# First stage of a hybrid diffusion layer on one core: the modulation from plain fp32 products, latents shifted and scaled by rows before the transposes, tokens loaded in between

## The chip, the cores and the metric

The kernel runs on one core of a Trainium2 chip. The metric is device time in microseconds of one execution; the smaller the better. The core's engines are TensorE (PE in the views), VectorE (DVE), ScalarE (ACT), GpSimd (POOL) and the queue SP, which in this kernel issues nearly all transfers. Each engine works its instructions off in the order in which they were built into its queue.

## What is computed

One layer of a bidirectional diffusion backbone over 2048 latent tokens and 256 context tokens of width 1024. The part that matters here is the very first:

```python
c_act, cctx_act = silu(c), silu(c_ctx)
mod_lat = c_act @ ada_w + ada_b            # 6 x 1024, shift and scale are the first two parts
mod_ctx = cctx_act @ ada_w + ada_b
h_ctx = rmsnorm(ctx, norm1_g) * (1 + csc1) + csh1
h_lat = rmsnorm(x + pos, norm1_g) * (1 + sc1) + sh1
proj  = h @ w_in                           # for both, then three groups of heads, a gated residual and an MLP
```

Everything behind `proj` (recurrent, linear-attention and mLSTM heads, output projection, MLP) makes up the other nineteen twentieths of the time and is not touched.

## The kernel before

All is fp32. To multiply exactly enough with TensorE's fast fp32 form (`F32R`), an operand is split into a part rounded to that form and the rest, and three products stand for one: `hTh` and `hTl` are the two parts of the normalised, modulated and transposed tokens, `whi` and `wlo` those of a weight block.

The stage before the heads runs like this. `csp` holds the two activated condition vectors (latents, context) in split form. For 8 row blocks k and 4 column blocks j a piece `aw` (128x512) of `ada_w` is loaded through SP into one of 8 slots (L271); ScalarE casts it to `awh` (L274), VectorE or GpSimd subtracts to get `awl` (L275), and two products (L276, L277) add it up in four PSUM banks `mps[j]`. The results are copied out as `mrow` and transposed, so that shift (`mT`) and scale (`sc1`) stand as one column for each of 8 blocks of 128 features.

Tokens come in 18 tiles of 128: two of the context (group 0) and four for each of the latent groups 1 to 4. `norm_in` loads a tile `xt` into one of 4 slots, adds the position for latents on GpSimd (`prow` in L237, `posc` in L238), sums squares on ScalarE (`junk`, L251), gets the reciprocal root from a few one-column operations (L215 to L225) and scales the tile on VectorE (L253). `modulate` transposes it in two halves of four blocks into PSUM `tp` (L444), applies scale and shift block by block into `hy`, five blocks of a tile on VectorE (L448) and three on ScalarE (L450), casts `hy` to `hTh` on ScalarE (L451) and subtracts to get `hTl`, one half on VectorE and one on GpSimd (L452).

TensorE's order is written out by hand: between the tiles a filler puts products of an earlier group (`first0` to `first4`, two weight blocks each, L365 to L367), some 2.7 us of them after each tile; `first4` stands behind all tiles. After it the first block of the long projection, `xa1`, begins. On the other engines a scheduler orders by data and by priorities (`tc.high_priority`); the modulation pieces have the highest. The weights of `first` (`wraw`, `whi`, `wlo`) are split on VectorE in the same stage.

## Time and profile before

| | |
|---|---|
| median of 3 runs | 2755.17 us (2750.44 to 2756.03) |
| the profiled execution: time | 2759.21 us |
| its span | 2757.4 us |
| busy in the span: TensorE, VectorE, ScalarE, GpSimd | 93%, 63%, 42%, 35% |
| the stage that is changed | about the first 150 us |

The shares are means over stages with different limits: TensorE's 93% says what bounds the kernel as a whole, not what bounds its first 150 us. The profiled execution is one run of the program, a little above the median; durations are taken from it, and a shift worked out from them is set against the median.

### The profile page before, as it was taken

Reading aid. Unit: us, or ns where it says so; the run is one execution under the profiler, and the core shown is the slowest. Engines: PE = TensorE matmul, PEld = TensorE weight load, DVE = VectorE, ACT = ScalarE, POOL = GpSimd, SP = SyncE. Lnnn points to the kernel's source line nnn. Section 1 sums busy time; section 2 is a strip of 40 time slices with the busy share of each in tenths; the row PEclk is TensorE's granted clock in tenths of the full one; section 3 lists DMA queues with packets and bytes.
Section 4 is the critical chain, followed back from the end, with each engine's and each line's share of the span. In section 5 each row is a group of like instructions: output and inputs, shape, how many; then the busy total and the mean of one; then the engine's idle time right before and its main releaser. Section 6 shows DMA issues by size and latency. Waiting matters only on the chain. (4 is left out here: it accounts for less than half of the span.)

```text
span 2757.4 us, 36372 instructions
## 1 busy us (share of the span) xinstructions
PE 2551.9 (93%) x12239; PEld 2074.5 (75%) x12239; DVE 1743.9 (63%) x3040; ACT 1159.9 (42%) x2052; POOL 972.6 (35%) x868
## 2 busy tenths in 40 slices
PE   5799999999998889788997999999999999999997
PEld 2677778888877667776775888878887887888876
DVE  7855476156648876746665776766665256555586
ACT  6746421233336665433334544544445322232343
POOL 5734411245444443424452333243331222222221
PEclk8999999999999999889998999999999999999999
DMA  7444365665656565856663776665555576656564
GB/s 222 143 133 120 99 183 168 167 156 162 159 156 172 169 188 176 275 182 207 209 203 115 207 221 203 197 192 145 157 149 158 186 263 224 212 179 198 171 206 153
DMA packets 490215, 495.24 MB, mean 180 GB/s; under 512 B 88226, under 2 KB 371580, under 8 KB 490028
## 3 DMA queue, kind: packets, MB, share of 16 engines
q1 hardware_dynamic: 464204, 465.45, 56.1%
q10 hardware_dynamic: 20352, 15.86, 1.8%
q0 software_dynamic: 5472, 11.60, 1.5%
q8 instruction: 97, 1.59, 0.2%
q14 instruction: 90, 0.74, 0.1%
HBM read 336.89 MB, written 155.92 MB: 179 GB/s over the span
## 5 line engine op out<-in xcount | busy, mean ns | idle before, releaser
L365 PE MATMUL pp<-hTh,whi 128*128 128x512 f32 (+1 forms) x1048 | 433.7, 414 | 12.8 <-DVE evt L505 8.8
L367 PE MATMUL pp<-hTh,wlo 128*128 128x512 f32 (+1 forms) x1048 | 406.4, 388 | 6.0 <-POOL wlo L313 3.9
L366 PE MATMUL pp<-hTl,whi 128*128 128x512 f32 (+1 forms) x1048 | 405.0, 386 | 0.2 <-DVE hTl L452 0.2
L1806 PE MATMUL yps<-bh,al 128*128 128x512 f32 x832 | 326.9, 393 | 6.6 <-DVE al L1425 3.5
L1804 PE MATMUL yps<-bh,ah 128*128 128x512 f32 x832 | 325.8, 392 | 0.0
L1805 PE MATMUL yps<-bl,ah 128*128 128x512 f32 x832 | 324.5, 390 | 0.0
L1425 POOL TENSOR_TENSOR al<-ar,ah 128x1024 fp32r<-128x1024 f32 x54 | 132.1, 2445 | 485.3 <-ACT ah L1666 448.6
L1666 ACT CAST ah<-ar 128x1024 fp32r<-128x1024 f32 x108 | 113.5, 1051 | 305.6 <-PE yps L1805 264.7
L365 PEld LDWEIGHTS pp<-hTh,whi 128*128 128x128 f32 x1048 | 203.5, 194 | 50.1 <-DVE evt L505 10.9
L367 PEld LDWEIGHTS pp<-hTh,wlo 128*128 128x128 f32 x1048 | 202.3, 193 | 49.8 <-POOL wlo L313 6.3
L366 PEld LDWEIGHTS pp<-hTl,whi 128*128 128x128 f32 x1048 | 203.5, 194 | 33.4 <-issue 1.9
L1806 PEld LDWEIGHTS yps<-bh,al 128*128 128x128 f32 x832 | 156.3, 188 | 46.5 <-DVE al L1425 8.5
L1805 PEld LDWEIGHTS yps<-bl,ah 128*128 128x128 f32 x832 | 156.3, 188 | 33.4
L1804 PEld LDWEIGHTS yps<-bh,ah 128*128 128x128 f32 x832 | 156.5, 188 | 31.9
L1498 PE MATMUL accy<-th,whi 128*128 128x512 f32 x384 | 153.1, 399 | 2.0 <-DVE tz L1428 1.9
L1500 PE MATMUL accy<-th,wlo 128*128 128x512 f32 x384 | 151.8, 395 | 1.6 <-DVE wlo L1425 1.6
L1425 DVE TENSOR_TENSOR wlo<-wab,whi 128x512 fp32r<-128x512 f32 x124 | 128.8, 1039 | 37.3 <-ACT whi L1433 37.3
L1499 PE MATMUL accy<-tl,whi 128*128 128x512 f32 x384 | 150.5, 392 | 0.0
L1433 ACT CAST whi<-wab 128x512 fp32r<-128x512 f32 x124 | 76.8, 620 | 131.9 <-PE accy L1499 57.4
L1428 POOL TENSOR_TENSOR uz<-tz 128x512 f32<-128x512 f32 x32 | 50.0, 1566 | 224.8 <-DVE tz L1428 144.6
L313 POOL TENSOR_TENSOR wlo<-wraw,whi 128x512 fp32r<-128x512 f32 x54 | 78.2, 1450 | 143.8 <-ACT whi L312 134.8
L1498 PE MATMUL pp<-th,whi 128*128 128x512 f32 x256 | 104.9, 410 | 15.9 <-ACT whi L1433 12.8
(407 smaller groups left out, 6008.5 us busy)
## 6 DMA issues: line engine op xcount, KB each, us to landing
uD<-uz SPq DMA_DIRECT2D x224, 256.0 KB
ar<-uD SPq DMA_DIRECT2D x108, 512.0 KB
braw<-in_mlp_w_dram SPq DMA_DIRECT2D x84, 512.0 KB
wab<-in_mlp_w_dram SPq DMA_DIRECT2D x62, 512.0 KB
maw<-in_ada_w_dram SPq DMA_DIRECT2D x64, 256.0 KB
wraw<-in_w_in_dram SPq DMA_DIRECT2D x54, 256.0 KB
rb<-rD SPq DMA_DIRECT2D x96, 128.0 KB
aw<-in_ada_w_dram SPq DMA_DIRECT2D x32, 256.0 KB
```

The lines of the kernel that those rows point to most:

```text
L313: (nc.vector if early else nc.gpsimd).tensor_tensor(lo, raw, hi.bitcast(F32), op=ALU.subtract)
L365: nc.tensor.matmul(acc[:, 0:n], hi, hTh[g][:, k, :], start=k == 0, stop=False)
L366: nc.tensor.matmul(acc[:, 0:n], hi, hTl[g][:, k, :], start=False, stop=False)
L367: nc.tensor.matmul(acc[:, 0:n], lo, hTh[g][:, k, :], start=False, stop=k == KC - 1)
L1425: eng.tensor_tensor(o, a, b, op=ALU.subtract)
L1498: nc.tensor.matmul(acc, hi[:, k, :], T2[i][0][:, k, :], start=first and k == 0, stop=False, skip_group_check=True)
L1499: nc.tensor.matmul(acc, hi[:, k, :], T2[i][1][:, k, :], start=False, stop=False, skip_group_check=True)
L1500: nc.tensor.matmul(acc, lo[:, k, :], T2[i][0][:, k, :], start=False, stop=k == 3, skip_group_check=True)
L1666: nc.scalar.copy(hi, r_)
L1804: nc.tensor.matmul(acc, ah[:, p_, :], bh, start=p_ == 0, stop=False)
L1805: nc.tensor.matmul(acc, ah[:, p_, :], bl, start=False, stop=False)
L1806: nc.tensor.matmul(acc, al[:, p_, :], bh, start=False, stop=p_ == 7)
```

## The change

The products of the modulation take `aw` as it is, in plain fp32, two columns of `cact` against 512 of `aw`; the split and `csp` go. The bias and the 1 of `1 + scale` are put in by four more products of a row of ones with the row `arow`. For the latents, shift and scale are taken as rows out of `mps` (the scale times `norm1_g`), spread over 128 partitions by four products of `ones1` with a row, and kept as `shB` and `scB`. A latent tile is then scaled and shifted before its transposes, by two operations of 128x1024 on VectorE, and `hTh` and `hTl` are taken straight out of PSUM, `hTl` on VectorE in both halves. For the context nothing changes in kind but its place: the tiles now come in the order of groups 1, 0, 2, 3, 4. The loads and norms of the first four tiles stand between the `aw` pieces from k = 2 on, with their priority.

```diff
-    csp = const.tile([P, KC, 4], F32R, name="csp")
-    nc.vector.tensor_copy(csp[:, :, 0:2], cact)
-    nc.vector.tensor_tensor(csp[:, :, 2:4], cact, csp[:, :, 0:2].bitcast(F32), op=ALU.subtract)
...
-        nc.vector.tensor_scalar(xt, xt, r0, r1, op0=ALU.mult, op1=ALU.mult)
-        return xt
-    tiles = [(g, j) for g in range(5) for j in range(GRP[g][1] // P)]
+        if g == 0:
+            nc.vector.tensor_scalar(xt, xt, r0, r1, op0=ALU.mult, op1=ALU.mult)
+            return xt, None
+        rs = nrm.tile([P, 1], F32, name="n1s", bufs=5)
+        nc.vector.tensor_tensor(rs, r0, r1, op=ALU.mult)
+        return xt, rs
+    tiles = [(g, j) for g in (1, 0, 2, 3, 4) for j in range(GRP[g][1] // P)]
...
-    for t_ in tiles[:NA]:
-        with tc.high_priority(PRI + 1000):
-            xts[t_] = norm_in(*t_)
+    hot.enter_context(tc.high_priority(PRI + 1500))
+    nc.vector.memset(ones1, 1.0)
+    nc.sync.dma_start(nrow, I["norm1_g"])
+    nc.sync.dma_start(arow, ada_b[0:2 * D].rearrange("(o n) -> o n", o=1))
+    nc.vector.tensor_scalar(arow[:, D:2 * D], arow[:, D:2 * D], 1.0, None, op0=ALU.add)
     for k in range(KC):
         for j in range(4):
-                nc.scalar.copy(ah, aw)
-                (nc.gpsimd if i % 5 in (0, 2) else nc.vector).tensor_tensor(al, aw, ah.bitcast(F32), op=ALU.subtract)
-            nc.tensor.matmul(mps[j][0:4, :], csp[:, k, :], ah, start=k == 0, stop=False)
-            nc.tensor.matmul(mps[j][0:2, :], csp[:, k, 0:2], al, start=False, stop=k == KC - 1)
+            nc.tensor.matmul(mps[j][0:2, :], cact[:, k, :], aw, start=k == 0, stop=False)
+        if 2 <= k < 2 + NA:
+            xts[tiles[k - 2]] = norm_in(*tiles[k - 2])
+    for j in range(4):
+        nc.tensor.matmul(mps[j][0:2, :], ones1[:, 0:2], arow[:, 512 * j:512 * j + 512], start=False, stop=True)
+    shB, scB = [sm.tile([P, D], F32, name=nm) for nm in ("shB", "scB")]
+    for j in (2, 0, 3, 1):
...
+            nc.vector.tensor_tensor(r_, mps[j][0:1, :], nrow[:, js], op=ALU.mult)
...
+            nc.scalar.copy(r_, mps[j][0:1, :])
+    for j in (2, 0, 3, 1):
...
+        nc.tensor.matmul(sb, ones1, rows[j])
+        (nc.vector.tensor_copy if j >= 2 else nc.scalar.copy)((scB if j >= 2 else shB)[:, js], sb)
...
-    def modulate(g, j, xt):
+    def modulate(g, j, xt, rs):
+        if g:
+            nc.vector.scalar_tensor_tensor(xt, xt, rs, scB, op0=ALU.mult, op1=ALU.mult)
+            nc.vector.tensor_tensor(xt, xt, shB, op=ALU.add)
...
+            y = tp
+            if g == 0:
+                y = nrm.tile([P, 4, P], F32, name="hy", bufs=1)
...
             nc.scalar.copy(hTh[g][:, ks, ts_], y)
-            (nc.gpsimd if hf else nc.vector).tensor_tensor(hTl[g][:, ks, ts_], y, hTh[g][:, ks, ts_].bitcast(F32), op=ALU.subtract)
+            nc.vector.tensor_tensor(hTl[g][:, ks, ts_], y, hTh[g][:, ks, ts_].bitcast(F32), op=ALU.subtract)
...
-        if g and j == 1:
-            fil.add(f"first{g - 1}", first(g - 1), GRP[g - 1][1] / 50)
+        if g != 1 and j == 1:
+            gp = {0: 1, 2: 0, 3: 2, 4: 3}[g]
+            fil.add(f"first{gp}", first(gp), GRP[gp][1] / 50)
```

The new operations have the lines L454 (scale), L455 (shift), L470 (`hTh`) and L471 (`hTl`) in the changed kernel; L212 to L222 and L248 are the norm's lines there, L234 and L235 the additions of `prow` and `posc`, L254 the product `rs` (tile `n1s`).

What this does to the order is shown at three places. The first is the SP queue at the start: before, all 32 `aw` pieces, then the position table `posc`, the small parameters and only then tokens.

```order
L271 DMA aw<-in_ada_w_dram 128x512 x32
L231 DMA posc<-in_pos_c_dram 128x512
L201 DMA pr<-in_head_norm_g_dram 8x128
L201 DMA pr<-in_lru_gate_b_dram 8x128
L201 DMA pr<-in_lru_lambda_dram 4x128
L201 DMA pr<-in_conv_w_dram 8x128
L201 DMA pr<-in_ada_b_dram 48x128
L201 DMA pr<-in_conv_b_dram 2x128
L201 DMA pr<-in_norm_g_dram 8x128 x2
```

Now, from the 17th `aw` on (ahead of these rows stand twelve pieces, a tile, two `prow`, four pieces, a tile and two `prow`):

```order
L274 DMA aw<-in_ada_w_dram 128x512 x4
L244 DMA xt<-in_x_dram 128x1024
L233 DMA prow<-in_pos_r_dram 64x512 x2
L274 DMA aw<-in_ada_w_dram 128x512 x4
L244 DMA xt<-in_x_dram 128x1024
L233 DMA prow<-in_pos_r_dram 64x512 x2
L274 DMA aw<-in_ada_w_dram 128x512 x8
L228 DMA posc<-in_pos_c_dram 128x512
```

The token loads moved ahead of the last pieces; `posc`, which the tokens need too, stayed behind the last.

The second place is VectorE where it turns from the modulation to the first token tiles. Before, `mT` and `sc1` are followed at once by the one-column operations (`n1v`, `n1t`) and the scaling of the first tile (`xt_127`).

```order
L285 COPY mrow_478<-m3_199 4x512
L292 TENSOR_TENSOR mT_491<-tr_459,prm_122 128x32
L294 TENSOR_TENSOR mT_491<-mT_491,tr_459 128x32
L297 SCALAR_TENSOR_TENSOR sc1_494<-mT_491,prm_122 128x16
L218 TENSOR_SCALAR n1v_135<-ss_129 128x1
L221 SCALAR_TENSOR_TENSOR n1t_137<-n1r_132,n1v_135 128x1
L225 TENSOR_SCALAR n1t_137<-n1t_137 128x1
L253 TENSOR_SCALAR xt_127<-xt_127,n1r_132,n1t_137 128x1024
L218 TENSOR_SCALAR n1v_149<-ss_143 128x1
L221 SCALAR_TENSOR_TENSOR n1t_151<-n1r_146,n1v_149 128x1
L448 TENSOR_SCALAR hy_552<-tp0_551,sc1_494,mT_491 128x128
L225 TENSOR_SCALAR n1t_151<-n1t_151 128x1
```

Now the first tile is `xt_174`, and `ss_277`, `n1r_280` and `n1v_283` belong to the fourth. The row of `n1s_256` belongs to the third.

```order
L215 TENSOR_SCALAR n1v_283<-ss_277 128x1
L454 SCALAR_TENSOR_TENSOR xt_174<-xt_174,n1s_192,scB_319 128x1024
L222 TENSOR_SCALAR n1t_253<-n1t_253 128x1
L218 SCALAR_TENSOR_TENSOR n1t_285<-n1r_280,n1v_283 128x1
L254 TENSOR_TENSOR n1s_256<-n1r_248,n1t_253 128x1
L299 COPY prm_119<-tr_336 128x128
L222 TENSOR_SCALAR n1t_285<-n1t_285 128x1
L327 CAST whi_401<-wraw_395 128x512
L254 TENSOR_TENSOR n1s_288<-n1r_280,n1t_285 128x1
L327 CAST whi_411<-wraw_405 128x512
L327 CAST whi_417<-evt_415 128x512
L328 TENSOR_TENSOR wlo_402<-wraw_395,whi_401 128x512
```

Behind these rows come two more `wlo`, one `mrow` and then the shift L455 of `xt_174`. One-column operations of the fourth tile and the splitting of the weights moved in between the first tile's two operations. What they wait for stands on ScalarE, where the squares of the third and fourth tile (`junk_246`, `junk_278`) now stand between copies of rows:

```order
L248 ACTIVATE junk_246,ss_245<-xt_238 128x1024
L213 ACTIVATE n1r_216<-n1r_216 128x1
L304 COPY mrow_340<-m0_127 2x512
L212 ACTIVATE n1r_248<-ss_245,epsc_120 128x1
L248 ACTIVATE junk_278,ss_277<-xt_270 128x1024
L213 ACTIVATE n1r_248<-n1r_248 128x1
L295 COPY shB_318<-pp_327 128x512
L212 ACTIVATE n1r_280<-ss_277,epsc_120 128x1
L295 COPY shB_318<-pp_333 128x512
L213 ACTIVATE n1r_280<-n1r_280 128x1
L304 COPY mrow_352<-m2_129 2x512
```

Two squares and the four short operations behind them stand ahead of the `n1r_280` that VectorE needs; the two halves of `shB` moved in between.

The third place is VectorE's work for one tile in the steady part. Before:

```order
L218 TENSOR_SCALAR n1v_1077<-ss_1071 128x1
L448 TENSOR_SCALAR hy_1096<-tp0_1095,sc1_494,mT_491 128x128 x2
L221 SCALAR_TENSOR_TENSOR n1t_1079<-n1r_1074,n1v_1077 128x1
L448 TENSOR_SCALAR hy_1136<-tp0_1135,sc1_494,mT_491 128x128
L225 TENSOR_SCALAR n1t_1079<-n1t_1079 128x1
L452 TENSOR_TENSOR hTl3_76<-hy_1084,hTh3_75 128x4x128
L253 TENSOR_SCALAR xt_1064<-xt_1064,n1r_1074,n1t_1079 128x1024
L448 TENSOR_SCALAR hy_1136<-tp0_1135,sc1_494,mT_491 128x128
L448 TENSOR_SCALAR hy_1148<-tp0_1147,sc1_494,mT_491 128x128 x2
L218 TENSOR_SCALAR n1v_1129<-ss_1123 128x1
L448 TENSOR_SCALAR hy_1148<-tp0_1147,sc1_494,mT_491 128x128
L448 TENSOR_SCALAR hy_1198<-tp0_1197,sc1_494,mT_491 128x128
```

Now:

```order
L215 TENSOR_SCALAR n1v_1097<-ss_1091 128x1
L455 TENSOR_TENSOR xt_975<-xt_975,shB_318 128x1024
L218 SCALAR_TENSOR_TENSOR n1t_1099<-n1r_1094,n1v_1097 128x1
L454 SCALAR_TENSOR_TENSOR xt_1036<-xt_1036,n1s_1054,scB_319 128x1024
L222 TENSOR_SCALAR n1t_1099<-n1t_1099 128x1
L471 TENSOR_TENSOR hTl4_370<-tp0_1106,hTh4_369 128x4x128
L254 TENSOR_TENSOR n1s_1102<-n1r_1094,n1t_1099 128x1
L471 TENSOR_TENSOR hTl4_370<-tp0_1113,hTh4_369 128x4x128
L455 TENSOR_TENSOR xt_1036<-xt_1036,shB_318 128x1024
```

Five `hy` pieces and the scaling L253 of a tile went; L454, L455, a second `hTl` and `n1s` came.

## Rows read from the trace of the kernel before

**Rows 1.** The page's head: span, and TensorE's busy time and share.

```profile
span 2757.4 us, 36372 instructions
...
PE 2551.9 (93%) x12239; PEld 2074.5 (75%) x12239; DVE 1743.9 (63%) x3040; ACT 1159.9 (42%) x2052; POOL 972.6 (35%) x868
```

**Rows 2.** TensorE's waits, 36 to 150 us: us in total, times, longest.

```profile
PE tp L444 <- DVE xt L253: 28.1, 10, 6.6
```

**Rows 3.** Windows: us, busy of each engine, granted clock, DMA share, GB/s.

```profile
3.00:29.00 26.00, 18.65 (x55) 3.04 (x56) 18.88 (x22) 18.06 (x30) 16.78 (x12) 1.00 0.94 316
73.70:132.30 58.60, 44.51 (x215) 36.28 (x216) 52.37 (x111) 46.07 (x112) 48.83 (x37) 0.88 0.49 152
```

**Rows 4.** TensorE's timeline: start us, us, instruction, [idle before <-releaser].

```profile
50.08 0.66 PE L444 MATMUL tp<-ident,xt 128*128 128x128 f32 x2 [6.62 <-DVE xt L253]
...
73.72 0.52 PE L444 MATMUL tp<-ident,xt 128*128 128x128 f32 x3 [3.15 <-DVE xt L253]
...
132.28 0.49 PE L444 MATMUL tp<-ident,xt 128*128 128x128 f32 x3
...
138.19 0.50 PE L365 MATMUL pp<-hTh,whi 128*128 128x512 f32 x1 [0.68 <-ACT hTh L451]
```

**Rows 5.** VectorE's groups, 73 to 132.3 us: busy us, mean ns | idle before.

```profile
L448 DVE TENSOR_SCALAR hy<-tp,sc,mT 128x128 f32<-128x128 f32 x53 | 19.3, 402 | 3.7 <-PE tp L444 2.2 <-POOL hTl L452 1.0
L253 DVE TENSOR_SCALAR xt<-xt,n1r,n1t 128x1024 f32<-128x1024 f32 x12 | 15.3, 1279 | 0.2
L452 DVE TENSOR_TENSOR hTl<-hy,hTh 128x512 fp32r<-128x512 f32 x11 | 13.3, 1210 | 0.0
L221 DVE SCALAR_TENSOR_TENSOR n1t<-n1r,n1v 128x1 f32<-128x1 f32 x11 | 5.6, 509 | 0.6 <-ACT n1r L216 0.6
L218 DVE TENSOR_SCALAR n1v<-ss 128x1 f32<-128x1 f32 x11 | 1.6, 145 | 1.4 <-ACT junk L251 1.4
```

**Rows 6.** Line L253: ns least/median/most, first and last start.

```profile
L253 DVE TENSOR_SCALAR xt<-xt,n1r,n1t x18: 799/1024/1794, 37.8 to 130.4; 128x1024 f32<-128x1024 f32 x18
```

**Rows 7.** Timeline of GpSimd and VectorE, 62 to 67.5 us.

```profile
61.66 1.26 POOL L238 TENSOR_TENSOR xt<-xt,posc 128x512 f32<-128x512 f32 x1
...
62.42 0.53 DVE L221 SCALAR_TENSOR_TENSOR n1t<-n1r,n1v 128x1 f32<-128x1 f32 x1 [0.81 <-ACT n1r L216]
...
67.32 0.21 DVE L221 SCALAR_TENSOR_TENSOR n1t<-n1r,n1v 128x1 f32<-128x1 f32 x1
```

**Rows 8.** VectorE's groups of the whole span, two shapes.

```profile
L1425 DVE TENSOR_TENSOR al<-ar,ah 128x1024 fp32r<-128x1024 f32 x54 | 65.9, 1220 | 21.9 <-ACT ah L1666 21.8
...
L1425 DVE TENSOR_TENSOR tl<-tr,th 128x512 fp32r<-128x512 f32 x28 | 16.9, 688 | 0.0
```

**Rows 9.** GpSimd's groups, 73 to 132.3 us.

```profile
L452 POOL TENSOR_TENSOR hTl<-hy,hTh 128x512 fp32r<-128x512 f32 x12 | 18.7, 1555 | 7.5 <-ACT hTh L451 7.3
L237 POOL TENSOR_TENSOR xt<-xt,prow 128x512 f32<-128x512 f32 x11 | 15.0, 1360 | 2.3 <-DMA prow<-in_pos_r_dram 2.3
L238 POOL TENSOR_TENSOR xt<-xt,posc 128x512 f32<-128x512 f32 x10 | 14.6, 1458 | 0.5 <-DMA xt<-in_x_dram 0.5
```

**Rows 10.** Timeline of TensorE: plain fp32 products of L574.

```profile
170.16 3.14 PE L574 MATMUL qk<-xc,gw 128*128 128x256 f32 x8 [3.54 <-DMA xc<-xcD]
...
211.00 3.60 PE L574 MATMUL qk<-xc,gw 128*128 128x512 f32 x8
```

**Rows 11.** Timeline of the SP queue: issues of aw and posc.

```profile
1.92 24.98 SPq L271 DMA_DIRECT2D aw<-in_ada_w_dram  x32
26.95 0.42 SPq L231 DMA_DIRECT2D posc<-in_pos_c_dram  x1
```

**Rows 12.** ScalarE's groups, 34 to 50 us.

```profile
L251 ACT ACTIVATE junk<-xt 128x1024 bf16<-128x1024 f32 x4 | 4.2, 1052 | 0.9 <-POOL xt L237 0.8
...
L215 ACT ACTIVATE n1r<-ss,epsc 128x1 f32<-128x1 f32 x4 | 1.1, 286 | 0.1
...
L285 ACT COPY mrow<-m 4x512 f32<-4x512 f32 x1 | 0.6, 574 | 2.4 <-PE tr L287 2.4
```

More of the change, by code (lines that the diff above doesn't have):

```diff
@@ L257, in body @@
     xts = {}
     NA = 4
-    for t_ in tiles[:NA]:
-        with tc.high_priority(PRI + 1000):
-            xts[t_] = norm_in(*t_)
     pm0 = psum(adst, "pm0")
     mps = [pm0.tile([P, 512], F32, name=f"m{i}") for i in range(4)]
+    nrow, arow, ones1 = [adp.tile([1, w_], F32, name=f"row{i}") for i, w_ in enumerate((D, 2 * D, P))]
+    hot = ExitStack()
+    hot.enter_context(tc.high_priority(PRI + 1500))
+    nc.vector.memset(ones1, 1.0)
+    nc.sync.dma_start(nrow, I["norm1_g"])
+    nc.sync.dma_start(arow, ada_b[0:2 * D].rearrange("(o n) -> o n", o=1))
@@ L266, in body @@
+    nc.vector.tensor_scalar(arow[:, D:2 * D], arow[:, D:2 * D], 1.0, None, op0=ALU.add)
     for k in range(KC):
         for j in range(4):
-            i = 4 * k + j
-            with tc.high_priority(PRI + 1500):
-                aw = adp.tile([P, 512], F32, name="aw", bufs=8)
-                nc.sync.dma_start(aw, ada_w[k * P:(k + 1) * P, 512 * j:512 * j + 512])
-                ah = adp.tile([P, 512], F32R, name="awh", bufs=3)
-                al = adp.tile([P, 512], F32R, name="awl", bufs=3)
-                nc.scalar.copy(ah, aw)
-                (nc.gpsimd if i % 5 in (0, 2) else nc.vector).tensor_tensor(al, aw, ah.bitcast(F32), op=ALU.subtract)
@@ L276, in body @@
[L276 to L277 removed]
+            aw = adp.tile([P, 512], F32, name="aw", bufs=8)
+            nc.sync.dma_start(aw, ada_w[k * P:(k + 1) * P, 512 * j:512 * j + 512])
+            nc.tensor.matmul(mps[j][0:2, :], cact[:, k, :], aw, start=k == 0, stop=False)
+        if 2 <= k < 2 + NA:
+            xts[tiles[k - 2]] = norm_in(*tiles[k - 2])
@@ new lines, in body @@
+    for j in range(4):
+        nc.tensor.matmul(mps[j][0:2, :], ones1[:, 0:2], arow[:, 512 * j:512 * j + 512], start=False, stop=True)
+    shB, scB = [sm.tile([P, D], F32, name=nm) for nm in ("shB", "scB")]
+    rows = {}
+    for j in (2, 0, 3, 1):
+        js = slice(512 * (j % 2), 512 * (j % 2) + 512)
+        rows[j] = r_ = arow[:, 512 * j:512 * j + 512]
+        if j >= 2:
+            nc.vector.tensor_tensor(r_, mps[j][0:1, :], nrow[:, js], op=ALU.mult)
+        else:
+            nc.scalar.copy(r_, mps[j][0:1, :])
@@ L444, in modulate @@
                 nc.tensor.transpose(tp[:, k, :], xt[:, (4 * hf + k) * P:(4 * hf + k + 1) * P], ident)
-            for k in range(4):
-                kk = 4 * hf + k
-                if k < 2 + hf:
-                    nc.vector.tensor_scalar(y[:, k, :], tp[:, k, :], sc1[:, kk, s:s + 1], mT[:, kk, s:s + 1], op0=ALU.mult, op1=ALU.add)
-                else:
-                    nc.scalar.activation(y[:, k, :], tp[:, k, :], AF.Identity, scale=sc1[:, kk, s:s + 1], bias=mT[:, kk, s:s + 1])
+            y = tp
+            if g == 0:
+                y = nrm.tile([P, 4, P], F32, name="hy", bufs=1)
+                for k in range(4):
+                    kk = 4 * hf + k
+                    if k < 2 + hf:
+                        nc.vector.tensor_scalar(y[:, k, :], tp[:, k, :], sc1[:, kk:kk + 1], mT[:, kk:kk + 1], op0=ALU.mult, op1=ALU.add)
+                    else:
+                        nc.scalar.activation(y[:, k, :], tp[:, k, :], AF.Identity, scale=sc1[:, kk:kk + 1], bias=mT[:, kk:kk + 1])
             nc.scalar.copy(hTh[g][:, ks, ts_], y)
-            (nc.gpsimd if hf else nc.vector).tensor_tensor(hTl[g][:, ks, ts_], y, hTh[g][:, ks, ts_].bitcast(F32), op=ALU.subtract)
+            nc.vector.tensor_tensor(hTl[g][:, ks, ts_], y, hTh[g][:, ks, ts_].bitcast(F32), op=ALU.subtract)
     for i, (g, j) in enumerate(tiles):
```

25 lines of the change are left out of this document (11 added, 14 removed).

## The prediction, made before the changed kernel ran

> **What bounds the kernel now.** The page's head comes first: TensorE is busy 93% of a span of 2757.4 us [rows 1], so whatever moves TensorE's products moves the end. The built order of every engine is the same in both kernels from the first `xa1` product on; the change lies wholly in the first 150 us. So I ask for that stage alone: what does TensorE wait for there? Its list of waits over 36 to 150 us is nearly one entry, the transposes of L444 waiting 28.1 us in ten places for the token tile `xt` that VectorE scales in L253 [rows 2]. The windows agree: from 73.7 to 132.3 VectorE is busy 52.37 of 58.60 us, ScalarE 46.07, TensorE 44.51 [rows 3]. The stage runs at VectorE's pace. TensorE's timeline gives the milestones: the first latent tile, third of eighteen, is transposed at 50.08, the seventh at 73.72, the last at 132.28, and `first4`, the products of the last group, starts at 138.19 [rows 4]. Eleven tiles from 73.72 to 132.28 are 5.32 us each. All that follows is in the same order in both kernels, so I carry the shift of `first4`'s start unchanged to the end.
>
> VectorE's groups over 73 to 132.3 show what a tile costs it: five hy pieces of 0.40, one scaling of 1.28, one hTl half of 1.21 and three short ones of 0.15, 0.51 and about 0.15 [rows 5]. The scaling has a minimum of 0.80 [rows 6] and a half of the size of hTl costs 0.69 where nothing disturbs it [rows 8]; the short product L221 costs 0.21 in one place and 0.53 in another, where it ends only when a GpSimd addition that began 0.76 us earlier does [rows 7]. So VectorE loses time to GpSimd: (1.28-0.80) x12 + (1.21-0.69) x11 + (0.51-0.21) x11 = 14.8 us over 33 GpSimd operations [rows 5, 9], 0.45 us for each, 1.35 a tile.
>
> **The change part by part.**
> *Products as plain fp32.* Gone are 32 casts on ScalarE, 32 subtractions on VectorE and GpSimd and 64 products; new are 32 plain products, four with one row for the bias, four that spread a row over 128 partitions. The trace has plain fp32 products in L574: four of 512 columns are eight records in 3.60 us, 0.90 each; four of 256 columns, right after a wait of 3.54 us, take 3.14, which for 512 columns is 1.57 each [rows 10]. With the first `aw` issued at 1.92 [rows 11] and the first product near 5 us, 32 end at 34 or at 55. I take 0.90 for all but the first few, since the stream is denser than the split products are now. But then the loads set the pace. Between 3 and 29 us the queue moves 316 GB/s [rows 3] for 8.4 MB of `aw`, and the last `aw` is issued at 26.9 [rows 11]. Now 2.1 MB of tokens and 1.0 MB of `prow` stand among them: 11.5 MB at 316 are 36.5 us, so with a start at 2 to 3 the last product ends near 39. The freed casts buy nothing here, because they lay beside the loads.
>
> *The table posc.* It still stands behind the last `aw`, so it lands near 40. Until then GpSimd can't finish any of the four early token tiles. Its first L235 ends at 41.3 (1.26 each [rows 7]), and ScalarE then has four tiles in its queue, a square of 1.06 and two short ones of up to 0.29 each, with `m0`, `m1`, one `mrow` and the two halves of `shB` between them, 0.57 each [rows 12]: 4 x 1.64 + 5 x 0.57 = 9.4, up to 51. VectorE's queue, as the order above shows, holds the first L454 behind `n1v_283` and the first L455 behind `n1t_285`, both of the fourth tile; so it can't run ahead of ScalarE. After 51 come seven pieces of 512 columns, weight parts and `mrow` (0.69 at most, 4.8) and a few short ones (1.0), then L455. The first transposes come at 58, where before two context tiles were done and the first latent one came at 50.08.
>
> *From there to the seventh tile.* VectorE has three L454 and three L455, eight hTl, two L253, two hy, the last weight piece and about a dozen short ones. L454 and L455 are of a form that the stage doesn't show; the nearest row is a two-input operation of 128x1024 at 1.22 [rows 8], the other end 1.22+0.52, that is with the loss that hTl shows. I take 1.22 and count the loss by itself. That is 19 us, less 0.06 for each of 35 operations that start before the one ahead has ended (below), 17, up to 75. The seventh tile's load waits for the third tile's slot, free near 70; then 0.77 MB at 316 GB/s (2.4), two additions, the square and its short ones: 77.5. L454, a context hTl and L455 (3.1) and three losses of 0.45 give 82, against 73.72.
>
> *The context tiles* were first and are now fifth and sixth. Eight hy and three hTl of theirs are still to come then, 8 x 0.40 + 3 x 0.69, less overlaps: 4.7.
>
> *A latent tile in the steady part.* Out: five hy (2.00), the scaling (0.80), one hTl half (0.69). In: L454 and L455 (2.44), two hTl halves read from PSUM (1.37; that form takes 0.69 in [rows 8]) and one short product (0.21). With the short ones that stay (0.51) the old list sums to 4.00 + 1.35 lost = 5.35, where the window has 52.37/11 = 4.76 busy [rows 3]. The difference, 0.59 over some 10 operations, is that each begins before the last has ended (a few evacuations, which the list leaves out, count against it); I take 0.06 each, 0.48 for the 8 operations of the new list. The gaps, 6.23/11 = 0.57, I leave. New: 4.53 - 0.48 + 0.57 = 4.62, and the loss to GpSimd, which now has two operations a tile instead of three: 0.90, so 5.52 against 5.32. For the loss the bounds are zero and all of GpSimd's 2.5 us.
>
> ScalarE loses three hy a tile and stays off the path. That `hy` and `csp` are gone costs nothing either way.
>
> **The sum.** 82 + 4.7 + 11 x 5.52 = 147.4, less 1.2 (the two hTl that lie behind the last L455): the last tile is transposed near 146.2. Now `first4` follows 5.91 us later, 0.68 of them a wait for hTh [rows 4]; the 18 products between stay, and by their end both hTl are there, so that wait goes: 146.2 + 5.2 = 151.4 instead of 138.19, 13 us later. The profiled execution took 2759.21 for its span of 2757.4, 4 above the median of the runs; 2755.17 + 13 = **2768 us**, 0.5% slower. About 0.2% (5.5 us) is what a measurement of this kernel can tell from no change.
>
> **The rivals.**
> *Not slower: the loss to GpSimd goes away.* GpSimd no longer writes hTl, two hTl halves a tile come from PSUM, and its two additions may fit beside these (2.5 us beside 1.4 and the short ones: only partly). A tile then costs 4.62. That takes 0.90 x 11 and some 2.5 before the seventh tile, 12.4, from the sum: +1, 2756. With the gaps gone too (0.57 x 11 more) it is -5.5, 2750. It decides from a loss below 0.2 us an operation. For it: the hy pieces, from PSUM too, stay at 0.40 in the window in which the scaling waits [rows 5]. Against: over half of the new VectorE time is in operations of the kind that waited, where before it was under half.
> *The lock in full.* If no work lies beside GpSimd's, a tile costs 2 x 1.26 + 4.62 = 7.1, 1.6 more for each of 11: +31, 2786. For it: L454 and L455 stand near each other, and the disturbed L221 lasted until GpSimd's addition ended [rows 7]. Against: the measured 0.45 is a third of an addition. The Trainium skill, page SBUF — State Buffer, section Who interferes with whom, states such a lock: GpSimd and a VectorE operation with two SBUF inputs exclude each other for a whole instruction, and the loser is blocked. By that rule alone this rival would be the forecast; the trace agrees on the lock, and disagrees on how often it bites.
> *Front earlier.* posc is small, and its parts might pass the `aw` in flight and land near 35; then the tile work hangs on the products, ScalarE is done near 47, and all is 4 to 5 us earlier: +8.5, 2764.
> *The products at the slow price.* At 1.57 throughout, as if TensorE stayed slow as after a wait, they would end at 55, and 16 us more come on top: +29, 2784. Against: L574's 0.90 came in a dense stretch, and the plain products are dense once the loads lead.
>
> **How the numbers follow.** My sum 0.55; loss gone 0.20, half of that with the gaps gone too; front earlier 0.11; lock in full 0.10; slow products 0.04. My sum by itself covers 2759 to 2777 (4.5 us on the front, 0.4 a tile). Faster: the half of the first rival without gaps, 0.10. Same: most of its other half (0.08), the low end of my sum (0.05) and of the early front (0.02), 0.15. Slower: 0.75. The range 2754 to 2786 cuts off the faster half of the first rival, half of the full lock and part of the slow products, under 0.2.
>
> **What the profile after would show.** Last plain product at 37 to 41, at 0.45 a record; the first L235 only after 39; the first transposes of a latent tile at 55 to 60; TensorE's waits there still for VectorE, now for L455; L454 and L455 at means of 1.4 to 1.6 with minima of 1.22; hTl at 0.69 throughout; seventh tile near 82, last near 146. I am wrong if the tiles come less than 5.1 us apart, if the first comes before 53, or if a later wait swallows the 13 us.

## The result, and the profile after

The changed kernel takes **2794.32 us** (median of 3 runs, 2791.53 to 2804.02) against 2755.17: ratio 1.0138, 95% interval 1.0115 to 1.0161, 39 us slower. 2768 was forecast, with a range up to 2786. The sign was right and the size a third of what came. The profiled execution is the longest of the three (2804.02).

The page's head, where [rows 1] showed 2757.4 and 2551.9:

```profile
span 2802.2 us, 36129 instructions
...
PE 2607.0 (93%) x12255; PEld 2088.4 (75%) x12255; DVE 1722.7 (61%) x2994; ACT 1126.4 (40%) x1976; POOL 931.8 (33%) x837
```

TensorE is 55 us busier, though its work behind the stage is the same. Its timeline in the stage (start us, us, instruction, [idle before <-releaser]), against [rows 4]:

```profile
36.18 8.72 PE L275 MATMUL m<-aw,cact 128*2 128x512 f32 x16 [2.06 <-DMA aw<-in_ada_w_dram]
44.84 4.51 PE L279 MATMUL m<-row,row 1*2 1x512 f32 x8
49.28 7.19 PE L294 MATMUL pp<-row,row 1*128 1x512 f32 x8
...
62.52 1.94 PE L460 MATMUL tp<-ident,xt 128*128 128x128 f32 x8 [0.64 <-DVE xt L455]
...
92.00 1.09 PE L460 MATMUL tp<-ident,xt 128*128 128x128 f32 x4 [7.88 <-DVE xt L455]
...
161.63 1.03 PE L460 MATMUL tp<-ident,xt 128*128 128x128 f32 x8
...
166.69 0.39 PE L380 MATMUL pp<-hTh,whi 128*128 128x512 f32 x1
```

The first latent tile is transposed at 62.52 (58 forecast), the seventh at 92.00 (82), the last at 161.63 (146.2), and `first4` starts at 166.69 (151.4; before 138.19). So at the end of the stage the kernel is 28.5 us behind, and the rest of the 39 (in this execution 44.8) comes in a part that the change does not touch. TensorE's waits from the start to 190 us (us in total, times, longest) name VectorE, as [rows 2] did, with `n1t` beside `xt`:

```profile
PE tp L460 <- DVE xt L455: 23.8, 8, 7.9
PE tp L460 <- DVE n1t L222: 9.3, 3, 3.9
PE m L275 <- DMA aw<-in_ada_w_dram: 7.2, 4, 2.1
```

VectorE's groups between the seventh and the last tile (busy us, mean ns | idle before), against [rows 5]:

```profile
L454 DVE SCALAR_TENSOR_TENSOR xt<-xt,n1s,scB 128x1024 f32<-128x1024 f32 x11 | 18.6, 1690 | 0.0
L471 DVE TENSOR_TENSOR hTl<-tp,hTh 128x512 fp32r<-128x512 f32 x22 | 14.7, 683 | 2.3 <-ACT hTh L470 2.2
L455 DVE TENSOR_TENSOR xt<-xt,shB 128x1024 f32<-128x1024 f32 x11 | 13.4, 1220 | 0.0
L218 DVE SCALAR_TENSOR_TENSOR n1t<-n1r,n1v 128x1 f32<-128x1 f32 x11 | 6.8, 622 | 0.1
...
L254 DVE TENSOR_TENSOR n1s<-n1r,n1t 128x1 f32<-128x1 f32 x11 | 2.7, 246 | 0.0
```

The windows (us, then busy of TensorE, its weight loads, VectorE, ScalarE, GpSimd, then granted clock, DMA share, GB/s) tell the same as [rows 3]: VectorE is busy 61.40 of 69.60, and the others are far from it. In the first window the granted clock is 0.67, a mean of the two levels 1.2 and 2.4 GHz; from 49.2 to 56.4 us, where the spreading products L294 run, it is 0.50, the lower level:

```profile
36.00:60.00 24.00, 22.25 (x45) 6.14 (x45) 8.53 (x29) 8.68 (x22) 7.00 (x7) 0.67 0.50 125
...
92.00:161.60 69.60, 48.85 (x244) 39.99 (x245) 61.40 (x102) 37.47 (x81) 32.58 (x22) 0.88 0.32 106
```

### The profile page after: what moved, and what is told of

Its sections match the earlier page's. It is cut to its first block, busy times and chain, and to the rows that moved or that the text cites. A ratio compares the mean times of both kernels' runs of the same rounds, so it can differ in the third digit from the quotient of the medians.

```text
span 2802.2 us, 36129 instructions
## 1 busy us (share of the span) xinstructions
PE 2607.0 (93%) x12255; PEld 2088.4 (75%) x12255; DVE 1722.7 (61%) x2994; ACT 1126.4 (40%) x1976; POOL 931.8 (33%) x837
## 5 line engine op out<-in xcount | busy, mean ns | idle before, releaser
L381 PE MATMUL pp<-hTl,whi 128*128 128x512 f32 (+1 forms) x1048 | 409.9, 391 | 0.0
L381 PEld LDWEIGHTS pp<-hTl,whi 128*128 128x128 f32 x1048 | 204.4, 195 | 36.2 <-issue 1.9
```

Of the source, the lines that this page charges most:

```text
L381: nc.tensor.matmul(acc[:, 0:n], hi, hTl[g][:, k, :], start=False, stop=False)
```

## Experiments

Medians of the runs and ratios to the kernel before on the same chip, which took 2753.0 to 2755.5 in the four series. The series are e1 to e4, e5 to e8, e9 to e12 and e13 to e15; differences across them are in medians and differ by some us from those by the ratios. "Left" and "right" are explained in the third part.

| run | what it is | us | ratio, 95% interval |
|---|---|---|---|
| e1 | the changed kernel again | 2798.95 | 1.0166 (1.0148 to 1.0184) |
| e2 | posc first | 2800.63 | 1.0171 (1.0152 to 1.0191) |
| e3 | bias products first | 2792.22 | 1.0138 (1.0121 to 1.0156) |
| e4 | latents modulated as before | 2781.47 | 1.0095 (1.0078 to 1.0113) |
| e5 | changed kernel, old addresses | 2779.93 | 1.0090 (1.0072 to 1.0108) |
| e6 | kernel before, new addresses | 2770.40 | 1.0059 (1.0039 to 1.0080) |
| e7 | e5, additions aside | 2765.75 | 1.0040 (1.0026 to 1.0054) |
| e8 | e5, additions aside and small | 2742.08 | 0.9960 (0.9944 to 0.9976) |
| e9 | before, plain products alone | 2758.90 | 1.0011 (0.9995 to 1.0027) |
| e10 | e4, old addresses | 2760.29 | 1.0017 (1.0002 to 1.0033) |
| e11 | before, left at 0 | 2769.28 | 1.0045 (1.0028 to 1.0062) |
| e12 | before, left at 480 | 2744.98 | 0.9958 (0.9937 to 0.9979) |
| e13 | before, both at 288 | 2746.53 | 0.9975 (0.9963 to 0.9988) |
| e14 | before, left 480, right 288 | 2770.63 | 1.0070 (1.0049 to 1.0090) |
| e15 | before, both at 480, lower | 2745.86 | 0.9980 (0.9968 to 0.9992) |

### The front: e1 to e4 and e9

**e1**, no edit. 

> The changed kernel once more, unedited. In its profiled execution first4's first product stood 28.05 us later than before (177.89 for 149.84), the shift then grew to 33 us near 900 us and to 45 at the end, and that execution was the longest of its three (2804.02, the others 2794.32 and 2791.53). Theory: the stage is what costs, 27 to 29 us of it again; a few us more (3 to 5) come up to 900 us; the rest, 33 to 45, is spread evenly over records that were 0.8 to 1.3 per cent longer in that one execution (L381 391 ns for 386) and doesn't come back: 2787 to 2796, records of the last products within 2 ns of before's. Rival: a later wait of the change's own making costs the 12 us; then it stands at one place, and the shift at the end is 40 us or more again.

(The product named there is the one behind `first4`'s last, in both kernels.) 2798.95, above the expectation, with an interval that overlaps the first one's. `first4` starts at 164.19, 26.0 late. The shift of one and the same product grows from 29.0 us (L381 at 652.91 for 623.87) to 40.2 (at 2747.37 for 2707.14). At 1500 us it is still 29.5; the rest comes behind that, a little in every stretch and at no one place. So neither side was right: not chance, and no wait.

**e2**: the one edit

```diff
-    with tc.high_priority(PRI + 1200):
+    with tc.high_priority(PRI + 1600):
         nc.sync.dma_start(posc, I["pos_c"])
```

> The changed kernel with one edit: the load of posc is issued ahead of the first aw instead of behind the last. Theory: VectorE's first L454 waited for scB, which is ready at 55.5 only since the spreading products L294 ended near 55; so the first latent tile comes at 60 to 62.5 (62.52 in the changed kernel), and the time falls by 0 to 4 us. Rival, the step of the prediction by which posc near 40 and ScalarE's four tiles behind it set the front: GpSimd's additions come at 17 to 32, ScalarE is done near 40, and the first latent tile comes near 54, 8 us earlier, all of it in the time.

The first addition of posc comes at 19.50 instead of 41.62, ScalarE has the four squares behind it at 40.2, and nothing is gained. Rows of e2's timeline:

```profile
19.50 1.26 POOL L235 TENSOR_TENSOR xt<-xt,posc 128x512 f32<-128x512 f32 x1 [19.05 <-DMA xt<-in_x_dram]
...
60.54 1.76 PE L460 MATMUL tp<-ident,xt 128*128 128x128 f32 x7
```

The forecast's mechanism for the front (posc, then ScalarE's four tiles) is refuted; its 58 was near the 60 to 62.5 measured for another reason.

**e3**:

```diff
+    for j in range(4):
+        nc.tensor.matmul(mps[j][0:2, :], ones1[:, 0:2], arow[:, 512 * j:512 * j + 512], start=True, stop=False)
     for k in range(KC):
...
-    for j in range(4):
-        nc.tensor.matmul(mps[j][0:2, :], ones1[:, 0:2], arow[:, 512 * j:512 * j + 512], start=False, stop=True)
```

> The changed kernel with one edit: the four products that add the bias row (L279, 4.51 us behind the last aw product, in series) come ahead of the first aw product, where TensorE waits anyway. Theory: TensorE's series behind the last aw (4.5 of bias, then the row copies, then 7.2 of spreading) holds scB and shB, so L294 and scB come 4 to 4.5 us earlier; the first latent tile follows by 2 to 4.5, and the time by 2 to 5. Rival (posc and ScalarE's four squares, done at 51, hold the front): the first tile moves by less than 1 us and the time by nothing that can be measured.

```profile
48.73 3.70 PE L296 MATMUL pp<-row,row 1*128 1x512 f32 x8 [0.35 <-DVE row L290]
...
56.68 1.97 PE L462 MATMUL tp<-ident,xt 128*128 128x128 f32 x8
```

These rows of its timeline show the first latent tile at 56.68, 3.4 us before e1's 60.05, as expected, but not for the reason expected. The spreading starts no earlier: 48.73, where e1 has 48.20. The bias products, now in front, hold back the first products and with them the slots of `aw`, so the last 16 records of L277 start at 39.65 instead of e1's 36.09. What became shorter is the spreading itself, 3.70 us (granted clock 1.00) for e1's 5.80 (0.63), and VectorE has the weight parts behind the first shift instead of in front of it. The time is 6.7 us lower than e1's, more than expected, though the two intervals touch; 2.7 of it are there at the last tile (156.46 for 159.12). What holds the front is TensorE's series of products, bias, row copies and spreading, then `scB` and VectorE's queue; what putting the bias first is worth by itself stays open. VectorE's rows of the changed kernel's timeline show the join:

```profile
54.80 0.69 DVE L295 COPY scB<-pp 128x512 f32<-128x512 f32 x1 [1.69 <-PE pp L294]
...
55.60 1.27 DVE L454 SCALAR_TENSOR_TENSOR xt<-xt,n1s,scB 128x1024 f32<-128x1024 f32 x1
...
61.17 1.20 DVE L455 TENSOR_TENSOR xt<-xt,shB 128x1024 f32<-128x1024 f32 x1
```

The first L454 starts when the last `scB` is copied; 4.3 us of weight parts and short operations stand between it and L455.

**e4**, core of the edit:

```diff
-            nc.vector.scalar_tensor_tensor(xt, xt, rs, scB, op0=ALU.mult, op1=ALU.mult)
-            nc.vector.tensor_tensor(xt, xt, shB, op=ALU.add)
...
+            y = nrm.tile([P, 4, P], F32, name="hy", bufs=3)
+            for k in range(4):
+                kk = 4 * hf + k
+                if k < 2 + hf:
+                    nc.vector.tensor_scalar(y[:, k, :], tp[:, k, :], sc1[:, kk, s:s + 1], mT[:, kk, s:s + 1], op0=ALU.mult, op1=ALU.add)
...
+            (nc.gpsimd if hf else nc.vector).tensor_tensor(
```

> The changed kernel with the latents modulated as before (scaled on VectorE, transposed, shift and scale by blocks from columns, hy, half of hTl on GpSimd); no shB, scB and no spreading products L294. What stays: plain products with the bias row, token loads among aw, posc behind them, the new order of groups. Theory: L454 and L455 on VectorE beside GpSimd's additions are what costs in the tiles (6.33 us a tile for 5.32), and the spreading holds the front; so the pace returns to 5.2 to 5.5, the first latent tile comes at 55 to 58, and the time is 4 to 10 us above before's, some 30 below the changed kernel's. Rival (the front's loads and products make the loss, the modulation little): the pace between the seventh and the last tile stays near 6.3 or the time stays 20 us or more above before's.

```profile
50.48 3.68 PE L460 MATMUL tp<-ident,xt 128*128 128x128 f32 x16
...
141.94 0.50 PE L380 MATMUL pp<-hTh,whi 128*128 128x512 f32 x1 [0.48 <-ACT hTh L468]
```

In TensorE's timeline the first latent tile comes at 50.48, where before had 50.08, and `first4` starts at 141.94, only 3.75 late; the seventh to the last tile are 5.34 us apart, as before. So the shift by rows makes some 22 to 25 of the stage's 26 to 28.5 us: theory right on the cause, though the first latent tile came earlier than its 55 to 58. And yet the time is 28 us above before. By time alone the rival would have won, since 4 to 10 us above it were expected; the trace says that some 24 us arise behind the stage.

**e9**:

```diff
-                nc.scalar.copy(ah, aw)
-                (nc.gpsimd if i % 5 in (0, 2) else nc.vector).tensor_tensor(al, aw, ah.bitcast(F32), op=ALU.subtract)
-            nc.tensor.matmul(mps[j][0:4, :], csp[:, k, :], ah, start=k == 0, stop=False)
-            nc.tensor.matmul(mps[j][0:2, :], csp[:, k, 0:2], al, start=False, stop=k == KC - 1)
+            nc.tensor.matmul(mps[j][0:2, :], cact[:, k, :], aw, start=k == 0, stop=k == KC - 1)
```

> The kernel before with one part of the change alone: the 32 plain fp32 products in place of 64 split ones and their 64 casts and subtractions (bias added from its column as before); the bytes of csp stay reserved, so all addresses are those of before. Theory: the products are not what costs; they follow the aw loads, whose order is that of before, and end 1 to 4 us later than now, since one takes 0.9 to 1.1 us; the first latent tile is transposed within 3 us of 50.1, and the time is 2752 to 2760. Rival (slow products carry much of the loss): first latent tile at 54 or later and a time of 2764 or more.

```profile
29.58 4.46 PE L276 MATMUL m<-aw,cact 128*2 128x512 f32 x10
...
50.89 1.51 PE L444 MATMUL tp<-ident,xt 128*128 128x128 f32 x6 [6.42 <-DVE xt L253]
```

Its timeline: five products in 4.46, 0.89 each, done at 34.0, the first latent tile 0.8 us later than before. Alone the plain products cost nothing that can be measured (interval from 0.9995).

### The tiles: e7 and e8

Both rest on e5 (next part) and leave out the position part of the tokens. The edit of e7, and in e8 the same on 8 columns instead of 512:

```diff
-        nc.gpsimd.tensor_tensor(xt[:, 0:512], xt[:, 0:512], prow, op=ALU.add)
-        nc.gpsimd.tensor_tensor(xt[:, 512:1024], xt[:, 512:1024], posc, op=ALU.add)
+        nc.gpsimd.tensor_tensor(prow, prow, posc, op=ALU.add)
+        nc.gpsimd.tensor_tensor(prow, prow, posc, op=ALU.add)
```

> The changed kernel with the 224 bytes, and GpSimd's two additions for a token tile go to prow (prow + posc, twice) instead of to the tile: left out is the position part of the tokens; GpSimd does as much as before, but nobody waits for it. Theory: tiles then cost what VectorE's list and the disturbance by GpSimd make of it; with the waiting for additions gone, the pace between the seventh and the last tile falls from 6.33 to 5.3 to 5.8 us, L454 stays above 1.45 in the mean, and the time is 5 to 12 us below that of the changed kernel with the 224 bytes. Rival: the latency of load, addition and square does not matter (VectorE is the bound): the time moves by less than 3 us.

> As the run with the additions aside, but each addition covers 8 columns instead of 512 (left out: the position part of the tokens, and GpSimd's work for it). What differs from that run is only how long GpSimd is busy beside VectorE. Theory: the loss to GpSimd, 0.90 us a tile in the prediction, is real and larger than that: L454 falls to 1.22 to 1.30 and L455 to 1.20 to 1.25, the tile by 0.8 to 1.5, and the time by another 10 to 18 us. Rival (loss to GpSimd small): L454 and the time stay within 3 us of the run with the additions aside.

The edit also reaches 16 tiles of the output stage, which use the same function, so the stage is read by its tiles. The last is transposed at 161.29 in e5, at 151.53 in e7 and at 139.25 in e8: 9.8 us for the waiting on the additions, 12.3 for GpSimd's being busy (beside VectorE, and with the slots of `prow` that the loads of later tiles queue for; the two were not taken apart). VectorE's groups between the seventh and the last tile, e7:

```profile
L455 DVE TENSOR_TENSOR xt<-xt,shB 128x1024 f32<-128x1024 f32 x11 | 14.5, 1319 | 0.0
L454 DVE SCALAR_TENSOR_TENSOR xt<-xt,n1s,scB 128x1024 f32<-128x1024 f32 x10 | 13.1, 1309 | 0.0
L254 DVE TENSOR_TENSOR n1s<-n1r,n1t 128x1 f32<-128x1 f32 x10 | 4.4, 436 | 0.0
L218 DVE SCALAR_TENSOR_TENSOR n1t<-n1r,n1v 128x1 f32<-128x1 f32 x10 | 4.2, 416 | 0.0
```

and e8:

```profile
L454 DVE SCALAR_TENSOR_TENSOR xt<-xt,n1s,scB 128x1024 f32<-128x1024 f32 x11 | 14.0, 1276 | 0.0
L455 DVE TENSOR_TENSOR xt<-xt,shB 128x1024 f32<-128x1024 f32 x11 | 13.4, 1217 | 0.0
L218 DVE SCALAR_TENSOR_TENSOR n1t<-n1r,n1v 128x1 f32<-128x1 f32 x11 | 2.3, 211 | 0.3 <-ACT n1r L213 0.3
...
L254 DVE TENSOR_TENSOR n1s<-n1r,n1t 128x1 f32<-128x1 f32 x11 | 1.7, 151 | 0.0
```

e8 gives the prices without a neighbour: 1.276, 1.217, 0.211 and 0.151. Against them the changed kernel loses (1690-1276) + (1220-1217) + (622-211) + (246-151) = 0.92 us a tile, where 0.90 was forecast, and over half of that in one-column operations. That the two agree is in part luck. GpSimd's rows of the changed kernel between the seventh and the last tile:

```profile
L235 POOL TENSOR_TENSOR xt<-xt,posc 128x512 f32<-128x512 f32 x8 | 16.2, 2022 | 0.0
L234 POOL TENSOR_TENSOR xt<-xt,prow 128x512 f32<-128x512 f32 x8 | 13.6, 1703 | 25.1 <-DMA xt<-in_x_dram 15.7 <-DVE n1t L218 4.8 <-DVE n1v L215 4.6
```

Only 16 additions lie in these eleven tiles, not two for each tile, since those of the tiles ahead came before; 10.1 us over 16 is 0.63 for each, where 0.45 was forecast. The additions themselves take 1.70 and 2.02 in the mean for 1.26 undisturbed. The hTl halves out of PSUM lose nothing (683 ns with GpSimd's additions, 684 without in e8). e7 met its pace (5.58 us a tile; L454 at 1.31 is below the 1.45 expected) and went a little beyond its time (14.2 us under e5, of which 9.8 are this stage's). e8 met the single prices; its pace fell by 0.5 only (5.07), since the loss sits as much in the first seven tiles, and of its 23.7 us under e7 only 12.3 are this stage's.

### Behind the stage: the addresses, e5, e6 and e10 to e15

The change takes `csp` and halves of `mT` and `sc1` out of the pool `const`, 224 bytes per partition. All long-lived tiles stacked behind it, the **left** side (`hTh`, `hTl`, later `th`, half of the slots of `bh`), begin 224 bytes lower; their start address has the remainder 64 by 512 instead of 288. The **right** side (`whi`, `wlo`, `evt`, later `ah`, `al`, the other half of `bh`) is stacked from the far end and stays at 480. Three quarters of the products of 512 columns take one operand from each side; nearly all the others take both from one side, and for them nothing changes. Nothing else differs between e5 and the changed kernel, nor between e6, e11 to e15 and the kernel before: instructions and their order are the same on every engine.

**e5**:

```diff
-    sgt = const.tile([P, 2 * KC], F32, name="sgt")
+    const.tile([P, 56], F32, name="pad"); sgt = const.tile([P, 2 * KC], F32, name="sgt")
```

> The changed kernel with one edit: 224 bytes per partition that nothing uses are reserved in the pool const, where csp and the halves of mT and sc1 lay that the change took out. All tiles on that side of SBUF (hTh, hTl, later woh, th, bh) then lie at the addresses that they had before, 224 bytes higher than in the changed kernel; the order on every engine is the same as in the changed kernel. Reason for it: the shift over before grows from 29 us near 620 us to 40 at the end in an undisturbed repetition, without a wait that explains it, and in the stretch from 1950 to 2100, in which TensorE is busy for all of 150.00 us in both, before passes 657 products and the changed kernel 645 (228 and 233 ns each). Theory: the address of the operands sets this pace; 657 products in such a stretch again, the shift at the end no larger than near 620 us (28 to 31), 2782 to 2788 us, 11 to 15 less than the changed kernel. Rival: the pace comes from something else of the change (what the queues carry, the state of the chip after the first stage): 645 products again and 2795 to 2801 us.

**e6**:

```diff
-    csp = const.tile([P, KC, 4], F32R, name="csp")
+    csp = sm.tile([P, KC, 4], F32R, name="csp")
...
+    const.tile([P, 24], F32, name="pad")
```

(`mT` and `sc1` are moved in the same way.) 

> The other way round: the kernel before with csp, mT and sc1 in the pool sm instead of const and 96 unused bytes in const, so that hTh and all tiles on that side lie 224 bytes lower, at the changed kernel's addresses. Order and work are those of before. Theory (addresses): about 645 products in a dense stretch of 150 us instead of 657, and 10 to 14 us longer than before, 2764 to 2768. Rival: as before, within 3 us.

TensorE in the windows (us, busy, products, clock, DMA share, GB/s): before,

```profile
1950.00:2100.00 150.00, 150.00 (x657) 1.00 0.48 137
```

the changed kernel,

```profile
1950.00:2100.00 150.00, 150.00 (x645) 1.00 0.53 150
```

e5,

```profile
1950.00:2100.00 150.00, 150.00 (x657) 1.00 0.52 148
```

and e6:

```profile
1950.00:2100.00 150.00, 150.00 (x644) 1.00 0.49 139
```

At full clock, never idle, and yet 644 or 645 products against 657, as the addresses have it. e5 takes 19.0 us off e1 (21 by the ratios), more than expected, and its shift no longer grows: 29.4 at 624 us, 24.3 at 2707. e6 puts 15.6 us on the kernel before, where 10 to 14 were expected.

**e10** is e4 with 32 words of padding in place of e5's 56. 

> The run with the old modulation in the changed kernel once more, now with 128 unused bytes in place of csp, so that hTh and its side lie where they lay before. That run was 27.9 us over before, though its first4 started only 3.9 us late, and it passed 230.25 ns a product in the dense stretch from 2220 to 2650 where before passes 228.1. Theory: the rest was the address; now 2756 to 2763, 18 to 25 us less, with 228 ns a product. Rival: the new order of groups and loads costs later in the kernel; then it stays above 2770.

2760.29, 21 us under e4, as the theory had it. The 230.25 and 228.1 in that text are mean distances between the starts of neighbouring `yps` products.

**e11 and e12** place the left side of the kernel before anew. e11 is e6 with 8 words for 24; e12 moves nothing and has

```diff
+    const.tile([P, 48], F32, name="pad")
```

> The kernel before with csp, mT and sc1 in the pool sm and 32 unused bytes in const: hTh and its side start at a multiple of 512 bytes (remainder 0; before has 288, the changed kernel 64, the run with the old modulation 160). Order and work are those of before. Both theories on how the address counts are open: if the distance to the operands on the other side (remainder 480 throughout) counts, 0 is near to 480 and differs from 64 little in itself; if only the tile's own start counts, a full multiple may be the best or the worst. Expected between 2735 and 2785, and the products in the stretch 1950 to 2100 (657 before, 644 at 64) move with the time.

> The kernel before with 192 unused bytes in const: hTh and its side have the remainder 480, the same as whi, wlo, ah and al on the other side. Order and work are those of before. If tiles with the same remainder hinder each other (both read at once by one product), this is the slowest address, 2770 or more; if they help, 2745 or less; if the remainder of the left side alone counts, anything between 2735 and 2785. The products in the stretch 1950 to 2100 move with the time.

e11 is slow (2769) and e12 fast (2745): of the cases named, the same remainder helps.

**e13 to e15**: e13 and e14 have the line below, which takes 48 words at the right end; e14 and e15 have `csp`, `mT` and `sc1` in `sm`, without padding in `const`.

```diff
+    spool(ctx, 'rpad').tile([P, 48], F32, name='rpad')
```

> The kernel before with 192 unused bytes at the far end of the other side of SBUF, where whi, wlo, ah, al and evt lie: their remainder by 512 falls from 480 to 288, that of hTh and its side stays 288. Order and work are those of before. So far, with 480 on the other side: 0, 64 and 160 slow (644 or 645 products in the stretch 1950 to 2100 at 0 and 64), 288 in between (657), 480 fast (662). If the two operands of a product do best at the same remainder, this is as fast as 480 with 480: 2742 to 2748, 661 products or more. If each side counts by its own remainder, the other side loses what the left side gains at 480: 2758 to 2770, 657 or fewer.

> The kernel before with hTh and its side at 480 (csp, mT and sc1 in the pool sm, nothing else) and the other side at 288. If the same remainder for both is what helps, this is slow, 2755 to 2770. If each side counts by itself, it lies by the loss of the other side above 2745, about as far above it as the run with 288 and 288 lies above 2755. Products in the stretch 1950 to 2100 move with it.

> Both sides at the remainder 480 again, but hTh and its side 512 bytes lower than in the run that had 192 unused bytes in const (csp, mT and sc1 moved to the pool sm). Theory: the remainder by 512 counts and not the place itself: 2740 to 2748, 661 to 663 products. Rival: how full const is or where the small tiles lie counts: 2752 or more.

The same window of e12,

```profile
1950.00:2100.00 150.00, 149.74 (x662) 1.00 0.50 143
```

of e13,

```profile
1950.00:2100.00 150.00, 148.13 (x652) 1.00 0.47 144
```

and of e14:

```profile
1950.00:2100.00 150.00, 150.00 (x645) 1.00 0.46 138
```

Busy time over products gives ns for one; e11, e4 and e15 have 645, 644 and 659 in 150.00, 150.00 and 149.57. A count takes in products that reach over an edge of the window, so these figures are a little low; the mean distance between the starts of neighbouring products in the window, which no edge touches, has three values only: 226.7 (e12, e13, e15), 228.9 (before, e5, e10) and 233.3 (e11, e6, e14, e4 and the changed kernel).

| runs | left, right | left less right, by 512 | ns a product | us (kernel before: 2753 to 2755) |
|---|---|---|---|---|
| e12, e15 | 480, 480 | 0 | 226.2, 227.0 | 2745, 2746 |
| e13 | 288, 288 | 0 | 227.2 | 2747 |
| before | 288, 480 | 320 | 228.3 | 2755 |
| e11 | 0, 480 | 32 | 232.6 | 2769 |
| e6 | 64, 480 | 96 | 232.9 | 2770 |
| e14 | 480, 288 | 192 | 232.6 | 2771 |
| e4 (changed kernel's stage) | 160, 480 | 192 | 232.9 | 2781 |

The relation of the two sides counts, not the remainder of one: 480 is the best left side against 480 and a bad one against 288, and 288 goes from middling to good when the right side comes to it. e13 met its time (its 652 products are below the 661 expected, since TensorE waits 1.87 us in this window); e14 lies at the upper end of its range; e15, with e12's remainders 512 bytes lower, is as fast within the intervals, so the place itself does not show. Other relations were not tried, and that 512 is the step after which they repeat rests on e15 alone.

One execution shows both paces side by side. The second part of the MLP multiplies blocks of `bh` that lie on the right and on the left by turns, with `ah` and `al` on the right. Two neighbouring blocks, right and then left, in the changed kernel (480 with 480, then 64 with 480):

```profile
2219.00:2259.00 40.00, 40.00 (x177) 1.00 0.55 171
2263.00:2303.00 40.00, 40.00 (x174) 1.00 0.76 248
```

and in e12 (480 with 480 in both):

```profile
2165.00:2205.00 40.00, 40.00 (x178) 1.00 0.54 173
2209.00:2249.00 40.00, 40.00 (x178) 1.00 0.78 253
```

The distance between starts is 226.7 and then 233.3 ns in the changed kernel, 226.7 twice in e12. Clock and instructions are the same, and the fuller DMA queues of the second block, which e12 has too, cost nothing there.

e12, e13 and e15 beat both kernels by nothing but where tiles lie, e12 by 0.2 to 0.6%.

## Why the prediction was wrong

- **"I carry the shift of `first4`'s start unchanged to the end": this step failed.** Order and work behind the stage are the same, but each product takes 1.9% longer in the dense stretch (233.3 ns for 228.9), since `hTh`, `th` and half of `bh` lie 224 bytes lower against `whi` and `ah`. It costs 15.6 us (e6 against before) to 19.0 (e1 against e5). Of the 13 forecast to 39 (45 in e1) this is the larger half of the miss, and neither the diff nor the order of instructions shows it.
- **The front.** Term: products end near 39, posc near 40 and ScalarE's four tiles up to 51 set the first transposes at 58. posc sets nothing (e2). The products end at 44.84, since the loads in between make TensorE wait four times, 7.2 us in all, and the last eight products take 1.09 each; then 4.51 of bias and 7.19 of spreading follow, which the sum had priced at nothing. The spreading alone takes 1.80 a product at granted clock 0.50, twice the 0.90 of [rows 10]. Result 60 to 62.5, 2 to 4.5 over.
- **From the first to the seventh tile**, 24 forecast, 28.6 (e1) to 29.5 measured. The seventh tile's load leaves at 74.95, when the third tile is transposed and its slot free; its additions start at 79.43 and four tiles of them follow without a gap. Every VectorE operation with both inputs in SBUF then waits for an addition's end. GpSimd's and VectorE's rows of the changed kernel's timeline:

```profile
83.18 2.50 POOL L235 TENSOR_TENSOR xt<-xt,posc 128x512 f32<-128x512 f32 x2
...
84.69 1.00 DVE L254 TENSOR_TENSOR n1s<-n1r,n1t 128x1 f32<-128x1 f32 x1
85.63 1.27 POOL L234 TENSOR_TENSOR xt<-xt,prow 128x512 f32<-128x512 f32 x1
85.79 2.19 DVE L454 SCALAR_TENSOR_TENSOR xt<-xt,n1s,scB 128x1024 f32<-128x1024 f32 x1
86.85 2.25 POOL L235 TENSOR_TENSOR xt<-xt,posc 128x512 f32<-128x512 f32 x1
...
87.90 1.75 DVE L471 TENSOR_TENSOR hTl<-hy,hTh 128x512 fp32r<-128x512 f32 x1
89.06 1.71 POOL L234 TENSOR_TENSOR xt<-xt,prow 128x512 f32<-128x512 f32 x1
...
89.64 2.22 DVE L455 TENSOR_TENSOR xt<-xt,shB 128x1024 f32<-128x1024 f32 x1
```

  Over their free prices (0.15, 1.28, 0.69, 1.22) these four lose 3.8 us, 1.35 was allowed; the other half of the 4.6 to 5.5 us over was not taken apart. GpSimd waits as well: its additions at 86.85 and 89.06 take 2.25 and 1.71 instead of 1.26. The Trainium skill, page SBUF — State Buffer, section Who interferes with whom, states that such a pair exclude each other for a whole instruction and that whoever issues first blocks the other; in these rows the trace agrees in both directions.
- **From there to the last tile**, 4.7 + 11 x 5.52 - 1.2 = 64.2 forecast, 69.6 (70.4 in e1) measured. The list was right: free prices 1.276 + 1.217 + 2 x 0.684 + 0.146 + 0.211 + 0.147 + 0.151 = 4.52 a tile for 4.53, and the loss 0.92 for 0.90, this one with luck (0.63 for each of 16 additions, not 0.45 for each of 22). Mis-sized are the idle time, 69.60 - 61.40 = 8.2 or 0.75 a tile for 0.57, and the evacuations left out of the list (2.2 us). Most of the rest are three hTl of the context at 1.05 for 0.69.
- **Rivals.** Lock in full, 2786, came nearest in the time and is not what happened: over eleven tiles VectorE lost 0.92 a tile, not 2.5. The loss to GpSimd gone: refuted, though e8 shows what it would have brought. Slow products: the last eight took 1.09, not 1.57; only the spreading was slow. Right was that the loads set the pace of the products, that plain products bring and cost nothing, that VectorE stays the bound and that the sign is slower.

In sum, in medians: 4.8 us for products, loads and the order of groups (e10; its interval reaches from 0.6 to 9), 19.6 for shift and scale as rows (e5 less e10), 19.0 for the addresses (e1 less e5).

## What to carry to other kernels

Before a shift is carried through work that "stays the same", compare where its operands lie: a few hundred bytes more or less in a long-lived pool move everything stacked behind it, and the check is a window in which TensorE never idles, products before and after. To put an elementwise step in front of the transposes makes it an operation with two SBUF inputs, which queues with GpSimd; the same step behind them reads PSUM and does not. A short series of small products behind a long one is on the path at its full price, and that price depends on the clock that TensorE has there; to move one of them in front can hold back the loads by as much as it frees (e3).
